# A hybrid encoder layer: inverse softmax sums spread by DMA and applied in attention, instead of by TensorE in the mixing stage

## The chip, the cores and the metric

The kernel runs on one core of one Trainium2 chip. The metric is the device time of one execution in microseconds (us). All data is float32; matmuls are taken as three products of rounded parts (high x high, high x low, low x high) to keep the precision.

## The reference

One layer of a streaming encoder for a prompt of 2048 frames (16 tiles of 128) and a sample group of 8 streams x 16 frames (one more tile). Every sub-layer is wrapped in RMS norms. What matters here is the mixer: half of its channels come from banded attention (8 heads of 64), half from a convolution, and both go through one output projection.

```python
def one_chunk(c):
    ...
    s = jnp.einsum("bqhd,bkhd->bhqk", qc, kc, ...) * scale + bias
    s = jnp.where(valid[None, None, None, :], s, NEG_INF)
    p = jax.nn.softmax(s, axis=-1)
    return jnp.einsum("bhqk,bkhd->bqhd", p.astype(vc.dtype), vc)
...
y = jnp.concatenate([att, c], axis=-1) @ w_out
...
x = x + rmsnorm(y, g_mix_post)      # then memory attention, then a SwiGLU FFN
```

The softmax divides each query's row by the sum of its exponentials. Since the values product is linear, the division can be made after it; the kernel does so for the prompt.

## The kernel before

The engines are TensorE (PE), VectorE (DVE), ScalarE (ACT), GpSimd (POOL), and the DMA queue issued by SyncE (SP). Each engine works through its instructions in one order. That order is set when the program is built: a scheduler simulates all engines with a cost model and gives each engine, at any moment, the ready instruction of highest priority (earlier in the program, mostly). On the chip an instruction whose input isn't there yet holds up everything behind it on its engine. Nearly all on-chip buffers are places at fixed offsets in a few large arenas (`Region().lay(arena, offset in KB, (tag, KB, buffers))`, or `.at(tag, KB, (arena, [offsets]))`); two tiles that share bytes wait for each other as their uses follow in the program.

The stages are: memory keys and values; input projections with the convolution; **attention**; the **mixing stage** (output projection, with the sample's cross-attention filled in between); cross-attention of the prompt; and the FFN.

`attention` walks over 128 units (8 heads x 16 query tiles). For each unit `scores` makes a score tile in PSUM, one DVE instruction (L793) adds the bias and finds the minimum of the negated scores, and ACT (L795) takes the exponential and accumulates the row sums into `self.sums[:, t, h]`, a tile with queries in the partitions. Four units later `transp` transposes the exponentials on PE and splits them into high and low parts; six units later, for each group of four tiles, `values` multiplies by the head's values. Its PSUM result has the channels in the partitions and 512 queries along the row. ACT copies one half out (L900), DVE adds the other and writes the unnormalised result to 64 partitions of `self.attT` (L902). Beside this, generators fill in the sample's attention (`sample`: POOL scales its softmax at L830, PE transposes that at L835), loads of the next head (`head_load`, issued by SP), and the output weights (`out_weights`, L277 and L278 split them).

The sums lie with queries in partitions, but `attT` has them along the row, so they have to be transposed and spread over the 64 channels of a head. Before the change this is done at the mixing stage's pace. `selectors` builds a 16 x 512 matrix of zeros and ones. `weigh(t)` inverts the 8 heads' sums of tile t, splits them into high and low parts (L964 to L967), transposes them on PE (L970) and copies them to SBUF (L973). `prep(t)` in `mixout` then spreads them over the channels by four PE matmuls with the selector (L1015), multiplies `attT` by the result on DVE (L1017), and splits that and the convolution's output `ct` into high and low parts (L1023, L1024). `weigh` runs for tiles 0 and 1 near attention's end, for the others two tiles ahead in the mixing stage.

`mixout` takes the sample tile first, then tiles 0 to 15: 48 matmuls a tile (`mm3h`, L291), k from 0 to 7, of which k = 0 to 3 need the attention half and k = 4 to 7 the convolution half. Its first tiles are prepared with raised priority, so that their matmuls can fill PE at attention's end. Two buffers hold `ct`, loaded by SP (L1008), three PSUM banks the output halves. The last two output weights (k = 6 and 7) take the place of the last head's values, so they are split only after the last `values` matmul.

The places that matter for the change:

```python
# attention's pool: fa is an arena of 32 KB per partition
.lay(fa, 0, ("qbd", 0.5, 2), ("osb", 0.5, 2)).lay(fa, 5, ("otmp", 2, 1), ...)
# mixing stage's pool: ff is the same arena
.at("ct", 2, (ff, [2, 10])).lay(ff, 0, ("an", 2, 1)).lay(ff, 5, ("po", 4, 1))
```

Of the kernel before, what the change touches and what calls it, by code (L numbers as in the profile page):

```python
# [17 lines left out]
P = 128  # L18
D = 1024
KC = D // P  # L20
NPT = 16
S_TILE = 16
H = 8
DH = 64
# [9 lines left out]
NEG = -1e30  # L34
RATE = 1.0
DEPTH = 2
WEIGH = (122, 124)
FROM = 2
F2 = 2
SLAST = NPT * (H - 1) + 4  # L40
# [96 lines left out]
class Build:  # L137
# [81 lines left out]
    def setup(self):  # L219
        nc, A = self.nc, self.A  # L220
        enter = lambda n, **kw: self.ctx.enter_context(self.tc.tile_pool(name=self.nm(n), bufs=1, **kw))
        self.const = enter("const")
        self.dpool = enter("dram", space=DRAM)
        sb, ps = enter("sb"), enter("ps", space=PSUM)
        self.sbF = Arena(sb.tile([P, 13120], F32, tag="f", name="sbf"))
        sbr = Arena(sb.tile([P, 22528], F32R, tag="r", name="sbr"))
        self.xctx = ExitStack()
        sx = self.xctx.enter_context(self.tc.tile_pool(name=self.nm("sx"), bufs=1))
        self.sbR = Joined(sbr, Arena(sx.tile([P, 5120], F32R, tag="x", name="sbx")))
        self.ps = Arena(ps.tile([P, 4096], F32, tag="p", name="psb"))  # L230
# [12 lines left out]
        self.hn = [self.dram(f"hn{g}", [P, 3, 7, 512]) for g in range(3)]  # L243
        self.af = [self.dram(f"af{g}", [P, NF // 2, 7, 3 * P]) for g in range(3)]
        self.vsamp = self.dram("vsampd", [P, 512])

    def bias_tables(self, pool):
        nc, A = self.nc, self.A
# [500 lines left out]
    def att_pools(self):  # L749
# [1 line left out]
        self.attp = (Region().lay(sbF, 34.5, ("kc", 4, 2), ("kt", 4.25, 1), ("pp", 1.5, 1), ("vn", 2, 1))  # L751
                     .at("z", 2.5, (fa, [24]), (fb, [0, 2.5, 5]), (fa, [9, 11.5, 14, 16.5]))
                     .lay(fb, 7.5, ("vc", 4, 2), ("nmx", 0.03125, 12), ("sm", 0.03125, 2))
                     .lay(fa, 0, ("qbd", 0.5, 2), ("osb", 0.5, 2)).lay(fa, 5, ("otmp", 2, 1), ("bs", 1.0625, 1)).lay(fa, 19, ("bt", 2.5, 2))
                     .lay(sbR, 0, ("q20", 8, 1), ("k20", 8, 1), ("kl0", 8, 1), ("q21", 8, 1), ("k21", 8, 1), ("kl1", 8, 1),
                          ("v20", 8, 1), ("ph1", 10, 1), ("pl1", 10, 1), ("v21", 8, 1))
                     .lay(sbR, 88, ("ph0", 10, 1), ("pl0", 10, 1)))
# [25 lines left out]
    def attention(self):  # L783
        nc, A = self.nc, self.A
# [100 lines left out]
                nc.vector.tensor_tensor(pl[:, a:b, :], pt[:, :b - a, :], ph[:, a:b, :].bitcast(F32), ALU.subtract)  # L885
            return quad

        def values(h, hd, t, quad):
            v2 = hd[3]
            po = self.t(ps_o, [P, 4, P], F32, "o")  # L890
            blocks = sorted(range(max(0, t - 4), t + 4), key=lambda j: j > t + 1)
# [1 line left out]
            for x, (src, j) in enumerate(ops):  # L893
# [8 lines left out]
            nc.vector.tensor_tensor(self.attT[rr, h // 2, t * P:(t + 4) * P], po[:DH].rearrange("p a b -> p (a b)"),  # L902
                                    tmp[:, :], ALU.add)

        units = [(h, t) for h in range(H) for t in range(NPT)]
        heads = {0: self.head0}
# [7 lines left out]
            qbds.append(qb)  # L914
        fill = iter(())
        self.wo_load = self.out_weights()
        zq, quads = {}, {}
        n = len(units)
        LT = 4
        LV = 6  # L920
        for i in range(n + LV + 1):
            if i < n:
                h, t = units[i]
# [10 lines left out]
            u = i - LV  # L934
            if 0 <= u < n and u % 4 == 3:
                h, t = units[u]
                values(h, heads[h], t - 3, quads.pop(u // 4))
            if i % NPT and (i % 2 == 0 or i > SLAST):
                next(fill, None)
            if i == n - NPT:  # L940
                self.selectors()
            if i in WEIGH:
                for _ in self.weigh(WEIGH.index(i), ps_t, "t"):
                    pass
            if i in (n - 13, n - 11, n - 9, n - 7):
                next(self.wo_load)

    def selectors(self):

        nc = self.nc  # L950
        pool = self.wp = Region().lay(self.fa, 27.5, ("eye", 0.03125, 1), ("rc", 0.03125, 2)).lay(
            self.sbR, 84, ("expand", 2, 1), ("rt", 0.5, 3), ("rs", 0.0625, 2))
        eye = self.t(pool, [2 * H, H], F32, "eye")
        nc.vector.tensor_tensor(eye[:, :], self.ident[:2 * H, :H], self.ident[:2 * H, H:2 * H], ALU.add)
        expand = self.t(pool, [2 * H, 4, 2, DH], F32R, "expand")
        nc.vector.tensor_copy(expand[:, :, :, :].rearrange("p a b d -> p (a b) d"),
                              eye[:, :].unsqueeze(2).to_broadcast([2 * H, H, DH]))
        self.expand = expand[:, :, :, :].rearrange("p a b d -> p a (b d)")
        self.rts = {}

    def weigh(self, t, ps, tag):
        nc, pool = self.nc, self.wp
        rc = self.t(pool, [P, H], F32, "rc", 2)
        nc.vector.reciprocal(rc[:, :], self.sums[:, t, :])  # L964
        rs = self.t(pool, [P, 2, H], F32R, "rs", 2)
        nc.vector.tensor_copy(rs[:, 0, :], rc[:, :])
        nc.vector.tensor_tensor(rs[:, 1, :], rc[:, :], rs[:, 0, :].bitcast(F32), ALU.subtract)  # L967
        yield
        pt = self.t(ps, [P, 512], F32, tag)
        nc.tensor.transpose(pt[:2 * H, :P], rs[:, :, :].bitcast(F32).rearrange("p a h -> p (a h)"),  # L970
                            self.ident[:, :])
        self.rts[t] = self.t(pool, [2 * H, P], F32R, "rt")
        nc.scalar.copy(self.rts[t][:, :], pt[:2 * H, :P])  # L973

    def out_weights(self):
        nc = self.nc
# [12 lines left out]
    def mixout(self, ctx):  # L989
# [16 lines left out]
        def prep(t):  # L1006
            ct = self.t(pool, [P, 4, P], F32, "ct", 2)
            nc.sync.dma_start(ct[:, :, :].rearrange("p a b -> p (a b)"), self.cs[t])  # L1008
            if t == S_TILE:
                att = self.attS[:, :, :]  # L1010
            else:
                rt = self.rts.pop(t)
                pt = self.t(ps_p, [P, 512], F32, "p")
                for j in range(4):
                    nc.tensor.matmul(pt[:, j * P:(j + 1) * P], self.expand[:, j, :], rt[:, :], start=True, stop=True)  # L1015
                an = self.t(pool, [P, 4, P], F32, "an", 1)
                nc.vector.tensor_tensor(an[:, :, :], self.attT[:, :, t * P:(t + 1) * P],  # L1017
                                        pt[:, :].rearrange("p (j q) -> p j q", q=P), ALU.mult)
                att = an[:, :, :]
            mh = self.t(pool, [P, KC, P], F32R, "mh", 2)  # L1020
            ml = self.t(pool, [P, KC, P], F32R, "ml", 2)
            for sl, src in ((slice(4, 8), ct[:, :, :]), (slice(0, 4), att)):
# [684 lines left out]
```

## Time and profile before

| what | value |
|---|---|
| median of 3 runs | 3013.76 us (3012.63 to 3015.66) |
| the profiled execution's own time | 3012.76 us |
| its span, first to last instruction | 3011.0 us |
| mean granted TensorE clock | 0.991 |
| HBM traffic | 366 MB read, 142 MB written, 169 GB/s over the span |

A span is what the profiler recorded between the first and the last instruction; the execution's time is 1.8 us more. In rows of the timeline the first number is the start in us from the span's start, the second the duration in us; L-numbers are lines of the kernel; `<-` in brackets names what ended the idle time before. PEld is PE's weight load, which overlaps its matmuls. `sbf`, `sbr`, `sbx`, `flexb` are the SBUF arenas, `psb` is PSUM. An entry such as `x16: 188/203/206` gives the count and the minimum, median and maximum duration in ns. A waits entry gives the us in total, the times and the longest.

### The profile page before, as it was taken

Reading aid. Unit: us, or ns where it says so; the run is one execution under the profiler, and the core shown is the slowest. Engines: PE = TensorE matmul, PEld = TensorE weight load, DVE = VectorE, ACT = ScalarE, POOL = GpSimd, SP = SyncE. Lnnn points to the kernel's source line nnn. Section 1 sums busy time; section 2 is a strip of 40 time slices with the busy share of each in tenths; the row PEclk is TensorE's granted clock in tenths of the full one; section 3 lists DMA queues with packets and bytes.
Section 4 is the critical chain, followed back from the end, with each engine's and each line's share of the span. In section 5 each row is a group of like instructions: output and inputs, shape, how many; then the busy total and the mean of one; then the engine's idle time right before and its main releaser. Section 6 shows DMA issues by size and latency. Waiting matters only on the chain.

```text
span 3011.0 us, 46007 instructions
## 1 busy us (share of the span) xinstructions
PE 2925.7 (97%) x16932; PEld 2676.2 (89%) x16932; DVE 2126.8 (71%) x3077; ACT 1354.8 (45%) x2726; POOL 1392.6 (46%) x1304
## 2 busy tenths in 40 slices
PE   8999999979999999999999999999999999999998
PEld 8999999968887887787888999999999999888786
DVE  6696895958885466435358888888788998556655
ACT  4545464658883344323234333433344444433433
POOL 0267495710013235235357565546555776424413
PEclk9999999989999999999999999999999999999999
DMA  8635255557744556324246333544334446756664
GB/s 305 241 112 183 92 162 161 170 153 184 191 132 164 176 194 212 109 75 137 95 151 227 119 136 117 200 156 152 133 136 157 140 144 208 253 174 209 224 198 164
DMA packets 196430, 500.09 MB, mean 166 GB/s; under 512 B 18981, under 2 KB 82989, under 8 KB 187875
## 3 DMA queue, kind: packets, MB, share of 16 engines
q1 hardware_dynamic: 185883, 461.09, 47.8%
q0 software_dynamic: 10320, 36.05, 3.1%
q8 instruction: 133, 2.18, 0.3%
q14 instruction: 94, 0.77, 0.1%
HBM read 365.97 MB, written 141.81 MB: 169 GB/s over the span
## 4 chain that ended last, share of the span: by engine, by line
PE 38%; DMA 4%; POOL 3%; issue 3%; DVE 2%; ACT 1%; SPq 0%; DVEq 0%; POOLq 0%; ACTq 0%
PE psb L285 12%; PE psb L284 12%; PE psb L283 12%; DMA sbf<-in_w_down_dram 2%; POOL sbf L1558 1%; PE psb L291 1%; DMA sbf<-x 1%; PE psb L1413 1%; DVE sbr L1619 0%; POOL sbf L340 0%; DVE sbr L1436 0%; DMA sbf<-in_w_gate_dram 0%; DMA sbf<-hn 0%; DMA hn<-sbf 0%; DVE flexb L1498 0%
## 5 line engine op out<-in xcount | busy, mean ns | idle before, releaser
L283 PE MATMUL psb<-sbr 128*128 128x384 f32 (+3 forms) x2808 | 944.3, 338 | 3.5 <-ACT sbr L319 1.1
L284 PE MATMUL psb<-sbr 128*128 128x384 f32 (+3 forms) x2356 | 807.6, 343 | 2.6 <-DVE sbr L320 2.4
L285 PE MATMUL psb<-sbr 128*128 128x512 f32 (+3 forms) x1848 | 634.3, 345 | 3.7 <-DVE sbr L1619 3.5
L283 PEld LDWEIGHTS psb<-sbr 128*128 128x128 f32 x2808 | 531.4, 190 | 33.5 <-ACT sbr L1618 2.4
L285 PE MATMUL psb<-sbr,sbx 128*128 128x384 f32 (+2 forms) x1484 | 478.3, 323 | 0.1
L284 PEld LDWEIGHTS psb<-sbr 128*128 128x128 f32 x2356 | 446.1, 189 | 29.2 <-DVE sbr L320 2.7
L285 PEld LDWEIGHTS psb<-sbr 128*128 128x128 f32 x1848 | 348.4, 189 | 33.4 <-DVE sbr L1619 6.9
L291 PE MATMUL psb<-sbr 128*128 128x512 f32 x1200 | 297.8, 397 | 4.3 <-POOL sbr L1271 1.5
L1436 DVE TENSOR_TENSOR sbr<-sbf,sbr 128x512 fp32r<-128x512 f32 x258 | 262.6, 1021 | 39.8 <-ACT sbr L1435 38.9
L1435 ACT CAST sbr<-sbf 128x512 fp32r<-128x512 f32 x258 | 159.3, 620 | 276.5 <-PE psb L284 234.6
L285 PEld LDWEIGHTS psb<-sbr,sbx 128*128 128x128 f32 x1484 | 281.4, 190 | 0.6 <-POOL sbx L278 0.4
L523 DVE SCALAR_TENSOR_TENSOR psb<-sbf,psb 128x768 f32<-128x768 f32 (+1 forms) x290 | 264.4, 912 | 6.2
L291 PEld LDWEIGHTS psb<-sbr 128*128 128x128 f32 x1200 | 223.6, 190 | 50.5 <-POOL sbr L1271 1.9
L1619 DVE TENSOR_TENSOR sbr<-sbf,sbr 128x384 fp32r<-128x384 f32 (+1 forms) x231 | 166.5, 743 | 92.6 <-ACT sbr L1618 91.3
L278 POOL TENSOR_TENSOR sbx<-sbf,sbr 128x1024 fp32r<-128x1024 f32 x60 | 152.9, 2551 | 81.3 <-ACT sbr L277 77.7
L1558 POOL TENSOR_TENSOR sbf<-sbf 128x512 f32<-128x512 f32 x77 | 107.6, 1401 | 167.9 <-DMA sbf<-in_w_down_dram 166.2
L1618 ACT CAST sbr<-sbf 128x384 fp32r<-128x384 f32 (+1 forms) x231 | 110.5, 497 | 164.9 <-PE psb L284 133.4
L533 POOL TENSOR_TENSOR flexb<-flexb,flexb 128x128 f32<-128x128 f32 (+1 forms) x180 | 167.1, 929 | 21.7 <-ACT flexb L532 12.1
L283 PE MATMUL psb<-sbr,sbx 128*128 128x384 f32 (+1 forms) x524 | 170.8, 327 | 2.5 <-ACT sbx L1435 1.8
L1435 ACT CAST sbx<-sbf 128x512 fp32r<-128x512 f32 x153 | 94.7, 620 | 163.4 <-PE psb L284 143.2
L1436 DVE TENSOR_TENSOR sbx<-sbf,sbx 128x512 fp32r<-128x512 f32 x153 | 154.5, 1012 | 17.9 <-ACT sbx L1435 17.5
L277 ACT CAST sbr<-sbf 128x1024 fp32r<-128x1024 f32 x98 | 102.5, 1050 | 108.2 <-PE psb L284 56.1
(339 smaller groups left out, 6159.7 us busy)
## 6 DMA issues: line engine op xcount, KB each, us to landing
af<-flexb SPq DMA_DIRECT2D x33, 1344.0 KB, 6.1
sbf<-in_w_down_dram SPq DMA_DIRECT2D x154, 256.0 KB, 3.8
sbf<-af SPq DMA_DIRECT2D x90, 384.0 KB, 3.9
sbf<-in_w_gate_dram SPq DMA_DIRECT2D x66, 512.0 KB, 3.4
sbf<-in_w_up_dram SPq DMA_DIRECT2D x66, 512.0 KB, 3.5
sbf<-x SPq DMA_DIRECT2D x49, 512.0 KB, 4.0
sbf<-in_w_in_dram SPq DMA_DIRECT2D x48, 512.0 KB, 4.2
sbr<-ks SPq DMA_DIRECT2D x28, 512.0 KB, 10.3
```

The source lines that it names most:

```text
L278: self.lo_engine.tensor_tensor(lo[:, :], wf[:, :], hi[:, :].bitcast(F32), ALU.subtract)
L283: nc.tensor.matmul(ps, lh, rh, start=start, stop=False, **kw)
L284: nc.tensor.matmul(ps, lh, rl, start=False, stop=False, **kw)
L285: nc.tensor.matmul(ps, ll, rh, start=False, stop=stop, **kw)
L291: nc.tensor.matmul(y[o], l, r[:, o * 512:(o + 1) * 512], start=start and x == 0, stop=stop and x == 2)
L523: nc.vector.scalar_tensor_tensor(acc if w < CW - 1 else o, src(w), cwt[:, j, w:w + 1], acc, ALU.mult, ALU.add)
L533: nc.gpsimd.tensor_tensor(o, o, v, ALU.add)
L1435: nc.scalar.copy(hs[j][:, :], src[j])
L1436: nc.vector.tensor_tensor(ls[j][:, :], src[j], hs[j][:, :].bitcast(F32), ALU.subtract)
L1558: nc.gpsimd.tensor_tensor(acc[:, :], acc[:, :], q[:, :], ALU.add if s > 0 else ALU.subtract)
L1618: nc.scalar.copy(ch[:, m], a[:, x, m])
L1619: nc.vector.tensor_tensor(cl[:, m], a[:, x, m], ch[:, m].bitcast(F32), ALU.subtract)
```

## The change

`inverse` inverts the four columns of sums of one head and one group of four tiles on DVE (128 x 4), writes them by a DMA to a row in DRAM in query order (512 runs of 4 bytes), and reads that row back by a second DMA into 64 partitions at once (`rb`, 64 x 512). It is called two units after the group's last scores. `values` then has one more instruction: POOL multiplies the 64 x 512 block of `attT` in place by `rb`. There is one `rb` buffer, at 2 KB of `fa`, and two small `rc` buffers at 4 KB. In the mixing stage `prep` takes `attT` as it is; `selectors`, `weigh` and everything that calls them go.

```diff
-WEIGH = (122, 124)
+        self.rec = [self.dram(f"rec{h}", [NPT * P]) for h in range(H)]
-                     .lay(fa, 0, ("qbd", 0.5, 2), ("osb", 0.5, 2)).lay(fa, 5, ("otmp", 2, 1), ...
+                     .lay(fa, 0, ("qbd", 0.5, 2), ("osb", 0.5, 2), ("rb", 2, 1), ("rc", 0.03125, 2)).lay(fa, 5, ("otmp", 2, 1), ...
-        def values(h, hd, t, quad):
+        def values(h, hd, t, quad, inv):
...
-            nc.vector.tensor_tensor(self.attT[rr, h // 2, t * P:(t + 4) * P], po[:DH].rearrange("p a b -> p (a b)"),
-                                    tmp[:, :], ALU.add)
+            att = self.attT[rr, h // 2, t * P:(t + 4) * P]
+            nc.vector.tensor_tensor(att, po[:DH].rearrange("p a b -> p (a b)"), tmp[:, :], ALU.add)
+            nc.gpsimd.tensor_tensor(att, att, inv[rr, :], ALU.mult)
+
+        def inverse(h, t):
+            rc = self.t(pool, [P, 4], F32, "rc", 2)
+            nc.vector.reciprocal(rc[:, :], self.sums[:, t:t + 4, h])
+            row = self.rec[h][t * P:(t + 4) * P]
+            nc.sync.dma_start(row.rearrange("(a p) -> p a", p=P), rc[:, :])
+            rb = self.t(pool, [P, 4 * P], F32, "rb")
+            rr = slice((h % 2) * DH, (h % 2 + 1) * DH)
+            nc.sync.dma_start(rb[rr, :], bass.AP(row.tensor, row.offset, [[0, DH], [1, 4 * P]]))
+            return rb
...
+        LR = 2
...
-                values(h, heads[h], t - 3, quads.pop(u // 4))
+                values(h, heads[h], t - 3, quads.pop(u // 4), invs.pop(u // 4))
+            u = i - LR
+            if 0 <= u < n and u % 4 == 3:
+                invs[u // 4] = inverse(units[u][0], units[u][1] - 3)
...
-            if i == n - NPT:
-                self.selectors()
-            if i in WEIGH:
-                for _ in self.weigh(WEIGH.index(i), ps_t, "t"):
-                    pass
...
-    def selectors(self):
-        ...
-    def weigh(self, t, ps, tag):
-        ...
 # mixout, prep
-                rt = self.rts.pop(t)
-                pt = self.t(ps_p, [P, 512], F32, "p")
-                for j in range(4):
-                    nc.tensor.matmul(pt[:, j * P:(j + 1) * P], self.expand[:, j, :], rt[:, :], start=True, stop=True)
-                an = self.t(pool, [P, 4, P], F32, "an", 1)
-                nc.vector.tensor_tensor(an[:, :, :], self.attT[:, :, t * P:(t + 1) * P],
-                                        pt[:, :].rearrange("p (j q) -> p j q", q=P), ALU.mult)
-                att = an[:, :, :]
+                att = self.attT[:, :, t * P:(t + 1) * P]
...
-            if 0 < i < len(order) - 2:
-                yield from self.weigh(order[i + 2], ps_p, "p")
```

More of the change, by code (lines that the diff above doesn't have):

```diff
@@ L753, in att_pools @@
                      .lay(fb, 7.5, ("vc", 4, 2), ("nmx", 0.03125, 12), ("sm", 0.03125, 2))
-                     .lay(fa, 0, ("qbd", 0.5, 2), ("osb", 0.5, 2)).lay(fa, 5, ("otmp", 2, 1), ("bs", 1.0625, 1)).lay(fa, 19, ("bt", 2.5, 2))
+                     .lay(fa, 0, ("qbd", 0.5, 2), ("osb", 0.5, 2), ("rb", 2, 1), ("rc", 0.03125, 2)).lay(fa, 5, ("otmp", 2, 1), ("bs", 1.0625, 1)).lay(fa, 19, ("bt", 2.5, 2))
                      .lay(sbR, 0, ("q20", 8, 1), ("k20", 8, 1), ("kl0", 8, 1), ("q21", 8, 1), ("k21", 8, 1), ("kl1", 8, 1),
@@ L916, in attention @@
         self.wo_load = self.out_weights()
-        zq, quads = {}, {}
+        zq, quads, invs = {}, {}, {}
         n = len(units)
@@ L936, in attention @@
                 h, t = units[u]
-                values(h, heads[h], t - 3, quads.pop(u // 4))
+                values(h, heads[h], t - 3, quads.pop(u // 4), invs.pop(u // 4))
+            u = i - LR
+            if 0 <= u < n and u % 4 == 3:
+                invs[u // 4] = inverse(units[u][0], units[u][1] - 3)
             if i % NPT and (i % 2 == 0 or i > SLAST):
                 next(fill, None)
-            if i == n - NPT:
-                self.selectors()
-            if i in WEIGH:
-                for _ in self.weigh(WEIGH.index(i), ps_t, "t"):
-                    pass
             if i in (n - 13, n - 11, n - 9, n - 7):
                 next(self.wo_load)
-    def selectors(self):
[L950 to L959, printed above, removed]
-    def weigh(self, t, ps, tag):
[L962 to L973, printed above, removed]
     def out_weights(self):
```

## The prediction

> **What bounds the kernel now.** I read the page first, then windows of the stretch in question, then the groups of that stretch, and last the timeline around single instructions.
>
> ```profile
> PE 2925.7 (97%) x16932; PEld 2676.2 (89%) x16932; DVE 2126.8 (71%) x3077; ACT 1354.8 (45%) x2726; POOL 1392.6 (46%) x1304
> ```
>
> TensorE (PE) is busy for 97% of the span, but that is an average; the change touches two stages only. The windows below (busy us of each engine, then granted clock, DMA share and GB/s) cover attention (about 642 to 926) and the mixing stage (from 898, overlapping, to about 1187).
>
> ```profile
> core 0: us, PE busy (x) PEld busy (x) DVE busy (x) ACT busy (x) POOL busy (x), PEclk, DMA share, GB/s
> ...
> 760.00:800.00 40.00, 39.04 (x296) 34.10 (x288) 35.08 (x85) 34.56 (x83) 2.69 (x6) 1.00 0.69 180
> 800.00:840.00 40.00, 39.85 (x320) 35.56 (x321) 33.41 (x84) 34.74 (x85) 1.49 (x4) 1.00 0.77 190
> ...
> 900.00:925.00 25.00, 24.55 (x137) 20.42 (x135) 15.96 (x28) 10.43 (x21) 5.85 (x4) 1.00 0.33 116
> 925.00:960.00 35.00, 31.38 (x118) 24.71 (x119) 16.85 (x25) 11.72 (x25) 11.26 (x16) 0.85 0.51 162
> ...
> 1080.00:1120.00 40.00, 40.00 (x215) 33.64 (x215) 29.27 (x37) 17.70 (x35) 16.32 (x30) 1.00 0.59 201
> ```
>
> The mixing stage is plainly bound by PE: 40.00 of 40 us, the other engines at three quarters or less, DMA at 0.6. So PE work taken out there is time taken off. Attention is also PE-first (39 to 40 of 40), but DVE and ACT stand at 84 to 88% and the DMA engines at 0.69 to 0.77, while POOL is nearly empty. The seam at 925 to 960 is the one place here with real PE idle time (3.6 us) and a lowered clock (0.85).
>
> **What leaves PE.** The groups of PE between 885 and 1165 us (busy us, mean ns):
>
> ```profile
> L291 PE MATMUL psb<-sbr,sbx 128*128 128x512 f32 x406 | 104.9, 403 | 2.1 <-DVE flexb L1066 2.1
> L1015 PE MATMUL psb<-sbr 16*128 16x128 f32 x64 | 11.0, 286 | 0.2 <-ACT sbr L973 0.2
> L970 PE MATMUL psb<-ident,sbr 128*16 128x128 f32 x16 | 4.4, 272 | 0.0
> ```
>
> and the timeline of PE around one of each:
>
> ```profile
> 1002.20 1.63 PE L291 MATMUL psb<-sbr 128*128 128x512 f32 x6
> 1003.76 0.66 PE L1015 MATMUL psb<-sbr 16*128 16x128 f32 x4
> 1004.34 0.50 PE L291 MATMUL psb<-sbr 128*128 128x512 f32 x1
> ...
> 991.21 3.35 PE L291 MATMUL psb<-sbr,sbx 128*128 128x512 f32 x14
> 994.40 0.27 PE L970 MATMUL psb<-ident,sbr 128*16 128x128 f32 x1
> 994.43 4.59 PE L291 MATMUL psb<-sbr,sbx 128*128 128x512 f32 x19
> ```
>
> Wide matmuls start 0.23 us apart (19 in 4.59 us). The last of the six before the spreading group therefore starts at about 1003.43 and would be followed at 1003.66; the next one comes at 1004.34, so a group of four costs 0.68 us: 16 x 0.68 = 10.9, which agrees with the 11.0 us of the group. The transpose hides in the pipeline: the next wide matmul starts at 994.43 where 994.39 was due, 0.05 us with rounding, 0.8 us for 16. I take 11.8 us off; the two busy times together, 15.4, are the upper end, and 9.5, with the five groups before 930 counted at a third because PE waits there anyway, the lower.
>
> DVE loses 16 each of the scaling, the inverse and two casts in the mixing stage, and ACT 16 copies. I cost that at nothing: PE covers it (DVE 29 of 40 us at most). If PE were not the bound there, scaling and inverse alone (min/median/max ns below) would be worth 16 x (0.683 + 0.203) = 14.2 us.
>
> ```profile
> L1017 DVE TENSOR_TENSOR flexb<-sbf,psb x16: 635/683/689, 908.4 to 1158.2; 128x512 f32<-128x512 f32 x16
> L964 DVE RECIPROCAL flexb<-sbf x16: 188/203/206, 866.7 to 1086.6; 128x8 f32<-128x8 f32 x16
> ```
>
> **What comes into attention.** There are 32 groups of four tiles (8 heads x 4). Each gets an inverse of 128x4 on DVE, two transfers on SP's queue, and one 64x512 product on POOL. The first score reductions of head 1 and of head 7 give a head's length, 179.7 / 6 = 29.9 us, and 1.87 us for one of its 16 units:
>
> ```profile
> 685.12 0.29 DVE L793 CUSTOM_DVE_ANT_0 flexb<-psb,flexb 128x128 f32<-128x128 f32 x1 [0.79 <-PE psb L866]
> ...
> 864.77 0.29 DVE L793 CUSTOM_DVE_ANT_0 flexb<-psb,flexb 128x128 f32<-128x128 f32 x1
> ```
>
> *DVE.* 32 x 0.19 us = 6.1 us on an engine at 84%. PE's longest wait in attention is for DVE:
>
> ```profile
> PE psb L866 <- DVE flexb L793: 10.0, 12, 5.1
> ...
> 671.22 0.44 DVE L793 CUSTOM_DVE_ANT_0 flexb<-psb,flexb 128x272 f32<-128x272 f32 x1 [5.26 <-DMA flexb<-toep]
> ```
>
> Between 0 (hidden by the two score buffers) and 6.1 us; 1.5 taken, since PE idles only some 2% there.
>
> *The transfers.* No row has a run of 4 bytes. Nearest in shape is the value store: 128 partitions x 4 runs of 512 bytes, 2.7 us to landing; one of them keeps the 16 DMA engines at 0.30 for 3 us, 0.9 us. The spread back (64 rows of 2 KB) lies near the 32 KB load with 2 KB rows.
>
> ```profile
> vs<-sbx SPq DMA_DIRECT2D x32, 256.0 KB, 2.7
> ...
> sbf<-vsampd SPq DMA_DIRECT2D x8, 32.0 KB, 3.3
> sbr<-ks SPq DMA_DIRECT2D x28, 512.0 KB, 10.3
> ...
> 201.00:204.00 3.00, 3.00 (x27) 3.00 (x26) 2.93 (x5) 1.84 (x3) 2.84 (x3) 1.00 0.30 87
> ```
>
> A pair thus takes 0.4 + 2.7 + 0.4 + 3.3 = 6.8 us unloaded. From the inverse (two units after a group's last scores) to its values (six) lie four units, 7.5 us: just in time. But each head begins with six loads of 512 KB (the keys land after 10.3 us), and a pair behind them comes some 7 us later (10.3 against 3.3). The sum takes the DMA engines' time of a pair from the store, 0.9 + 0.5 (half the bytes). The Trainium skill ("DMA: Bandwidth & Descriptors", "Specifications") says that under 512 B the engines read, modify and write; that speaks against the change. By it, as an estimate, the first transfer doubles to 1.8 us and the time comes out as in rival 3 below; no run here shows which holds.
>
> *Who waits for a late pair.* The second transfer waits at the head of SP's queue for the first to land and for the product before to leave the one `rb` buffer; behind it stand the loads of the next head, of the sample caches and of the output weights. The heads' loads are issued a whole head ahead: head 2's first keys here, while head 2 begins at about 685.1 + 29.9 = 715 and the keys land in 10.3 us. So SP may stall 10 us and more without harm.
>
> ```profile
> 682.17 0.45 SPq L780 DMA_DIRECT2D sbr<-ks  x1
> ```
>  On POOL the product waits for `rb` and the next instructions queue behind it. The one with little slack is L830, which scales the sample's softmax; PE transposes its result 0.16 us later, in order:
>
> ```profile
> 704.23 0.68 DVE L902 TENSOR_TENSOR sbf<-psb,flexb 64x512 f32<-64x512 f32 x1
> ...
> 707.90 0.97 POOL L830 TENSOR_SCALAR flexb<-flexb 128x272 f32<-128x272 f32 x1 [4.12 <-DVE flexb L829]
> ...
> 709.03 0.49 PE L835 MATMUL psb<-ident,flexb 128*128 128x128 f32 x3
> ...
> L1558 POOL TENSOR_TENSOR sbf<-sbf 128x512 f32<-128x512 f32 x77 | 107.6, 1401 | 167.9 <-DMA sbf<-in_w_down_dram 166.2
> ```
>
> The product itself, at 1.4 us, would run from 704.9 to 706.3 and be gone by then; 32 x 1.4 = 45 us lie in POOL's empty time. Late by 2 to 5 us it holds up PE 8 times: 0 to 20 us, 2 taken.
>
> *DVE against POOL.* The row that could show the two hindering each other:
>
> ```profile
> 900.80 0.69 DVE L1024 TENSOR_TENSOR sbr<-sbf,sbr 128x512 fp32r<-128x512 f32 x1 [0.47 <-PE psb L866]
> 901.04 2.72 POOL L278 TENSOR_TENSOR sbr<-sbf,sbr 128x1024 fp32r<-128x1024 f32 x1 [11.43 <-ACT sbr L884]
> 901.41 2.89 DVE L1024 TENSOR_TENSOR sbr<-flexb,sbr 128x512 fp32r<-128x512 f32 x1
> ...
> L793 DVE CUSTOM_DVE_ANT_0 flexb<-psb,flexb x136: 280/810/826, 643.0 to 904.2; 128x640 f32<-128x640 f32 x96, 128x256 f32<-128x256 f32 x8, 128x128 f32<-128x128 f32 x8, 128x512 f32<-128x512 f32 x8
> ...
> L278 POOL TENSOR_TENSOR sbr<-sbf,sbr 128x1024 fp32r<-128x1024 f32 x4 | 9.9, 2466 | 35.8 <-PE psb L896 14.9 <-ACT sbr L884 11.4 <-PE psb L866 7.2
> ```
>
> A DVE subtraction with both inputs in SBUF took 2.89 us instead of 0.69 while POOL worked; the score reduction, with one input in PSUM, never exceeded 0.826. The Trainium skill ("SBUF — State Buffer", on the shared port pair) says the pair is locked for a whole instruction, also by a DVE operation with two SBUF inputs; the trace agrees. By it attention's DVE work, one input in PSUM, is left alone; if every DVE instruction could be held, 32 x 1.4 = 45 us of DVE would be at stake, and the 0.826 excludes that, for three more of POOL's subtractions (2.4 us each) ran beside those 136. Only the last product, at the seam, meets two-input work: 0 to 1.3 us, 0.6 taken.
>
> **The seam.** This cost isn't named in the change. `rb` lies at 2 to 4 KB of the arena `fa`, exactly where the mixing stage has its first `ct` buffer, that of the sample tile, mixed first. Before, nothing in attention used that place and the load ran ahead:
>
> ```profile
> 671.89 0.33 SPq L1008 DMA_DIRECT2D flexb<-cs  x1
> ...
> 922.60 1.27 PE L896 MATMUL psb<-sbr 128*128 128x512 f32 x7
> ...
> 928.22 4.63 PE L291 MATMUL psb<-sbr 128*128 128x512 f32 x10 [0.69 <-DVE sbr L278]
> ...
> 936.73 7.37 PE L291 MATMUL psb<-sbr,sbx 128*128 128x512 f32 x24 [2.13 <-DVE flexb L1066]
> ```
>
> Now the load has to wait for the last product. From the end of the last values matmul (923.9, call it T): ACT's copy and DVE's sum (0.7 each) to T+1.4; POOL's last weight subtraction (2.4), which waits for the same matmul, to T+2.4; the product to T+3.8, issue 0.4, load 2.7 (as the store of the same 256 KB), ACT's cast 0.6: T+7.5. Before, the sample tile went on at 928.22, T+4.3, with 12 matmuls left (k = 6, 7); now 24 are left (k = 4 to 7), 5.5 us at 0.23, more while the clock is low. PE gets its banks back 3.9 us after their end: T+16.9 to T+19.9, against 936.73 = T+12.9. The 12 matmuls fewer ahead of T bring T forward by 2.8. Loss 1.2 to 4.2, plus up to 2.8 if the tail is not PE-bound and T doesn't move; 4 taken, 1 to 7 kept.
>
> **Sum**, against the profiled execution (3012.76 us: its span of 3011.0 and 1.8 around it; the median of the three runs is 1.0 higher): -11.8 + 1.5 + 2 + 0.6 + 4 = -3.7, and with the median 3010.1. I say 3010. What can be told from no change is 0.2%, 6 us: below 3007.7 is faster, above 3019.8 slower.
>
> **Rivals.**
> 1. *Everything is hidden*: pairs in time, and the tail's matmuls reordered so that `ct` costs its least. 3013.8 - 11.8 + 1.2 + 0.5 = 3004. For it: POOL's emptiness, loads issued a head ahead. Against: the seam's overlap in the code. Chance 0.35.
> 2. *Slower: L830 behind a late product.* From 2 us of lateness of `rb` beyond 706.5 on, PE stops at L835 once a head. At 3 us a head 24 us, with the other terms 3013.8 - 11.8 + 6.1 + 24 = 3032; it decides from about 1.5 us a head (3020). For it: 10.3 us landings. Against: L830 comes late in a head, after the burst. Chance 0.18.
> 3. *Slower: the DMA engines become the bound.* 0.77 of a 29.9 us head is 23.0 us; four pairs at 0.9 + 0.5 make 28.6, still under. If 4-byte runs cost twice a 512-byte run, 32.2: 2.3 us x 7 heads, 3010 + 16 = 3026. Chance 0.09.
> The forecast keeps 0.38.
>
> **How the numbers follow.** The range reaches from rival 1 with a little more taken off PE (3001) to rival 3 and the lower part of rival 2 (3027); it has room for the 2 or 3 us by which a new order of instructions, worked out for the whole program, can differ. Faster takes rival 1 (0.35); slower rivals 2 and 3 (0.27); within 0.2% the forecast.
>
> **What would show it.** In the changed profile: no 16-row matmuls; mixing windows still at 40 of 40, the stage some 8 us shorter from its first full tile on; `flexb<-cs` issued first near the last product instead of at 672; POOL some 45 us more; in attention, PE's waits for L793 slightly longer, and any at L835 new. I am wrong if the `rec` transfers land well past 5 us, if L830 starts right behind a product that waited for a DMA, if PE's idle time in attention grows by over 5 us, or if the seam costs nothing.

## The result, and the profile after

The changed kernel takes 3171.8 us (median of 4 runs, 3168.1 to 3178.3) where the kernel before, on the same chip, takes 3014.4: a ratio of 1.052, 95% interval 1.050 to 1.054. It is slower by some 157 us; 3010 us, and at most 3027, had been forecast. The profiled execution has a span of 3176.2 us, 165.2 more than before.

The windows of attention and of the start of the mixing stage in the changed kernel's trace (busy us of each engine, granted clock, DMA share, GB/s):

```profile
681.00:721.00 40.00, 25.76 (x145) 21.58 (x145) 18.87 (x50) 17.83 (x42) 3.30 (x5) 0.79 0.73 112
...
801.00:841.00 40.00, 32.31 (x214) 28.41 (x215) 26.03 (x66) 24.16 (x57) 6.51 (x8) 0.86 0.75 127
...
961.00:1001.00 40.00, 17.61 (x123) 15.47 (x122) 12.89 (x34) 13.68 (x31) 7.37 (x6) 0.68 0.41 71
...
1161.00:1201.00 40.00, 40.00 (x240) 34.51 (x239) 18.48 (x28) 16.70 (x33) 11.24 (x26) 1.00 0.60 204
```

The mixing stage is as full as it was. In attention PE is busy for 18 to 32 of 40 us (39 to 40 in the rows shown of before), and no other engine has taken its place: DVE and ACT are down too, POOL is nearly empty, and the DMA engines move less (71 to 127 GB/s, where it was 180 and 190) at a share of busy time of 0.73, 0.75 and 0.41 (before 0.69 and 0.77). A stage in which every engine is partly idle and none is full waits for something that takes long and uses little. Two PE lines give the stage's length: the row of the score matmuls, with their first and last start, and the timeline of PE at the seam:

```profile
L866 PE MATMUL psb<-sbr x448: 221/338/690, 641.0 to 1046.3; 128*128 128x384 f32 x72, 128*128 128x256 f32 x68, 128*128 128x128 f32 x7, 128*128 128x512 f32 x3
```

```profile
1077.77 2.08 PE L896 MATMUL psb<-sbr 128*128 128x512 f32 x9
...
1101.98 7.38 PE L291 MATMUL psb<-sbr,sbx 128*128 128x512 f32 x24 [3.67 <-DVE flexb L1041]
```

From the first score matmul to the end of the last values matmul 438.9 us pass; before, 281.8 (642.1 to 923.9). That is +157.1. From there to the mixing stage's second batch of 24 matmuls it is 22.1 us against 12.9: +9.2. All the rest of the program is 1.1 us shorter. So the loss lies in attention. Its waits (us in total, times, longest), between 640 and 1100 us:

```profile
POOL sbf L904 <- DMA flexb<-rec: 108.6, 11, 14.5
DVE flexb L909 <- DMA rec<-flexb: 86.7, 12, 12.6
...
PE psb L883 <- DVE sbx L885: 49.7, 7, 20.1
...
PE psb L835 <- POOL flexb L830: 30.0, 6, 10.3
...
PE psb L896 <- DVE sbf L903: 27.0, 3, 10.3
```

The two longest are waits for the two transfers; PE's three are for DVE and POOL, which stand in them. SP's queue, which is listed apart, stands at the second transfer until the first has landed:

```profile
SPq L914 <- DMA rec<-flexb: 124.1, 11, 15.9
```

One such stop, as the timeline of the changed kernel shows it:

```profile
704.80 0.36 SPq L911 DMA_DIRECT2D rec<-flexb  x1
...
715.77 0.18 DVE L909 RECIPROCAL flexb<-sbf 128x4 f32<-128x4 f32 x1 [11.41 <-DMA rec<-flexb]
715.86 0.65 DVE L903 TENSOR_TENSOR sbf<-psb,flexb 64x512 f32<-64x512 f32 x1
...
716.66 0.76 PE L896 MATMUL psb<-sbx,sbr 128*128 128x512 f32 x1 [10.27 <-DVE sbf L903]
```

The first transfer of a group goes out at 704.80. The inverse of a later group needs one of the two `rc` buffers, and gets it only when an earlier first transfer (here the one issued at 695.11) has landed; DVE stands for 11.4 us, with the sum of the values behind it, and PE behind that. Meanwhile none of the three has work that it can start. The sizes and the landing times of the transfers stand in the DMA issues of the stage (640 to 1100; median us to landing), and in the row of line 911, the first transfer:

```profile
sbr<-ks SPq DMA_DIRECT2D x28, 512.0 KB, 17.2
flexb<-rec SPq DMA_DIRECT2D x32, 128.0 KB, 4.8
rec<-flexb SPq DMA_DIRECT2D x32, 2.0 KB, 13.2
```

```profile
DMA to landing us min/median/max: 10.0/13.2/20.6
```

Two kilobytes take 13.2 us at the median, where the forecast had 2.7. The trace dates only some of the landings, 6 of these 32, so 10.0 is not the least of all: one that is not dated took some 8 us, as shown further down.

### The profile page after: what moved, and what is told of

Read it like the earlier page. It is cut to its first block, busy times and chain, and to the rows that moved or that the text cites. A ratio compares the mean times of both kernels' runs of the same rounds, so it can differ in the third digit from the quotient of the medians.

```text
span 3176.2 us, 46003 instructions
## 1 busy us (share of the span) xinstructions
PE 2952.1 (93%) x16852; PEld 2699.8 (85%) x16852; DVE 2108.3 (66%) x3043; ACT 1357.8 (43%) x2710; POOL 1432.4 (45%) x1336
```

## The experiments

Ratios are to the kernel before on the same chip, with 95% intervals. Line numbers move by a few between kernels: the first transfer is `rec<-flexb`, the second `flexb<-rec` or, where `rb` lies elsewhere, `sbr<-rec`.

**1. Without the transfers.** The edit: one tile of ones in the place of `rb`, and no call of `inverse`.

```
-                invs[u // 4] = inverse(units[u][0], units[u][1] - 3)
+                invs[u // 4] = ones          # 1.0, in rb's place
```

> This kernel is the changed one without its inverses and transfers: rb is filled once with ones, so the rows are multiplied by 1 and the softmax stays undivided; POOL's 32 products, the place of rb and the lighter mixing stage stay. Four theories for the 157 us. W (writes): the transfer in 4-byte runs lands after 10 to 21 us where I had put 2.7, and all that waits for it (DVE for an rc buffer, SP for the second transfer, POOL for rb) sets attention's pace. B (buffers): the slow write would do no harm if DVE didn't wait for one of two rc buffers. S (SP): the harm is that SP stands at the second transfer and the loads of the next head come late. N: it isn't the transfers but the products on POOL, the place of rb or the new order of instructions. W, B and S all expect 3003 to 3011 us here (11.8 off PE, 1 to 7 back at the seam); N expects over 3100.

Measured: 3014.3 us, ratio 0.9999 (0.9987 to 1.0011). The 157 us are gone, with 32 products still on POOL: the product, PE's order and the buffers' places are not what costs. But the time is that of the kernel before, not 3003 to 3011; where PE's saving went is question 4.

**2. Which wait?** Three edits of the changed kernel, one wait or one shape each:

```
e2:  -  rc = self.t(pool, [P, 4], F32, "rc", 2)          (region: "rc", 0.03125, 2)
     +                                                   (region: "rc", 0.03125, 16)
e3:  -  nc.sync.dma_start(row.rearrange("(a p) -> p a", p=P), rc[:, :])   # 512 runs of 4 B
     +  nc.sync.dma_start(row.rearrange("(p a) -> p a", a=4), rc[:, :])   # 128 runs of 16 B
        (and the product reads rb with a stride of 4)
e4:  both transfers on nc.gpsimd's queue instead of nc.sync's
```

> The changed kernel with 16 rc buffers instead of 2, so that DVE's inverse no longer waits for an earlier write to land. B expects nearly everything back: 3010 to 3040 us. W expects that only DVE's own wait goes (87 us of it in the list of waits, partly in parallel with others), while SP and POOL still wait: 3060 to 3140. S expects no change to speak of: 3150 and more.

> The changed kernel with the inverses written in the order in which they lie: 128 runs of 16 bytes instead of 512 of 4, the same 2 KB; the row is read back as before, and the product reads it with a stride of four. Number of transfers, buffers, queue and order of waits stay as they are. W expects the write to land in 3 to 6 us and 3005 to 3035 us in all. B expects the same only if landing is under the 14 us between inverses two apart, so no difference from W here. S, where the count of transfers and the stop on SP matter, expects the loss to shrink by less than half: over 3080. N expects about 3170, or more, since the product's read is strided.

> The changed kernel with both small transfers issued from POOL's queue instead of SP's; runs of 4 bytes and buffers as they are. S expects 3010 to 3050 us, since the loads are never behind a waiting transfer. W expects the landing to stay above 8 us and POOL to stand in SP's place, with L830 and the products behind it: 3120 to 3250. B expects DVE's wait for rc to stay and the time above 3100.

Measured: e2 3178.2 us (1.0542, 1.0505 to 1.0580), e3 3050.2 (1.0119, 1.0096 to 1.0142), e4 3188.6 (1.0577, 1.0536 to 1.0617). In e2 DVE's wait is gone from the list, and nothing is won (theory W had expected 3060 to 3140 us); its waits read

```profile
POOL sbf L904 <- DMA flexb<-rec: 143.8, 16, 14.5
...
PE psb L835 <- POOL flexb L830: 100.0, 6, 24.3
```

The same lateness comes out one step later: POOL waits longer for `rb`, L830 stands behind it, and PE waits for L830. In e4 the same waiting moves to POOL's own queue (73.7 us for the first transfers to land). So neither the two buffers nor SP's queue alone is the cause. The shape of the first transfer is: with a quarter of the runs it lands in 5.7 us (median) and 122 of the 157 us are back, though not all that theory W had expected (3005 to 3035 us).

**3. Load or lateness?** In e8 the first transfers are there, but nobody reads them and nothing waits for them (16 `rc` buffers; the products take constant ones). In e7 all is there, but the product comes one group later.

```
e8:  inverse() writes rec and returns the tile of ones; no second transfer
e7:  -  values(...)                    # ends with the product of this group
     +  late.append(values(...)); if len(late) > 1: weigh(*late.pop(0))
     both: 16 rc buffers, rb in 4 KB of sbR that nothing else uses
```

> The inverses and the first transfers (512 runs of 4 bytes) alone: nobody reads what they write, the products use constant ones (rows are not scaled by the sums), 16 rc buffers, ones in the unused 4 KB. Theory L: nothing waits for them, so the time is that of e1b plus DVE's 32 inverses, 3003 to 3015 us, though ks lands late. Theory C: 3060 to 3170 us, most of the loss of the changed kernel, since the loads behind and beside the writes come late.

> Runs of 4 bytes as in the changed kernel, but the product of a group is issued one group later (behind the next group's values, some 7.5 us more lead), with 16 rc and two rb buffers in the unused 4 KB. Theory L (lateness: the 162 us are engines that wait for a landing): most of it is hidden, 3003 to 3030 us, POOL's wait for rb under 30 us in all, DVE's none. Theory C (contention: the 512 runs hold up the DMA engines, and the loads of keys and tables with them): 3080 to 3170 us even so, with PE's waits for data of ks and toep.

Measured: e8 3073.6 us (1.0194, 1.0173 to 1.0215), e7 3192.4 (1.0584, 1.0557 to 1.0610). e8 falls into the lower end of theory C's range, e7 lies above both ranges. The bare transfers cost about 62 us against the same kernel without them (3011.1, below), though nobody waits for them: that is load. The rest of the loss, some 95 us, comes only where the transfers are read and waited for, and more time for the product alone does not help. (The two parts need not be the same in the changed kernel, where the DMA engines are busy for 65.6% of 640 to 1100 us; in e8 it is 99.9% of a stretch shown below.) The trace of e7 has the reason in SP's own waits:

```profile
SPq L917 <- DMA rec<-flexb: 285.5, 29, 14.7
```

In 29 of 32 groups SP stands at the second transfer until the first has landed. I then moved the second transfer a group later in the program as well (e10, and e11 with 16-byte runs).

```
e10, e11:  spread(h, row), the second transfer, is called beside the group's values, not in inverse()
```

> Runs of 4 bytes; the second transfer is issued one group after the first (beside that group's values, 7.5 us later), and the product another group after it; 16 rc and two rb buffers in the unused 4 KB. Theory Q (queue: each second transfer holds SP's queue until the first has landed, 10 to 13 us for a group every 7.5 us, and with it the next pair and the heads' loads): the stall goes and only the load on the DMA engines is left, as in the run with the writes alone: 3065 to 3100 us, with SP's waits for rec in the tens of us where e7 had 285. If the lateness of the product was the point, e7 would have helped already; if it is the transfers themselves in any order, 3150 to 3190 us.

> The same order as e10 with 128 runs of 16 bytes, which land in 5.7 us, under a group's 7.5. Theory Q: no stall of SP's queue is left, and little load: 3008 to 3022 us, as the kernel before or a little better. If runs of 16 bytes still load the DMA engines so that the keys come late, 3025 to 3040 us as e6.

Measured: e10 3189.9 us (1.0575, 1.0556 to 1.0594), e11 3034.0 (1.0060, 1.0041 to 1.0079). e10 did not test what it was meant to. Its SP wait is 285.5 us again, because the scheduler still put each second transfer ahead of the next group's first one, as this stretch of SP's queue in e10 shows:

```profile
726.83 0.45 SPq L920 DMA_DIRECT2D sbr<-rec  x1
727.37 0.54 SPq L914 DMA_DIRECT2D rec<-flexb  x1
...
737.64 0.45 SPq L920 DMA_DIRECT2D sbr<-rec  x1
...
738.82 0.42 SPq L914 DMA_DIRECT2D rec<-flexb  x1
```

First and second transfers take turns, so that one group cannot pass in less than one landing: 10 us and more, where attention has a group every 7.5. Only an explicit order parts them (e13; e14 with 16-byte runs):

```
e13, e14:  with self.tc.issue_after(<first transfer of the next group>):
               rbs[g] = spread(...)
```

> Runs of 4 bytes. e10 did not test theory Q: its trace shows each second transfer issued directly ahead of the next group's first one, so that the two still take turns on SP's queue, and SP waits 285 us for rec as in e7. Here each second transfer is put behind the next group's first transfer on the queue (and the product a group later), so that two first transfers land at the same time. Theory Q: SP's wait for rec falls from 285 us to under 130, the attention stage comes down to that of the writes alone: 3065 to 3110 us. If the queue is not what costs the other 100 us: 3150 to 3190 us again.

> The order of e13 with 128 runs of 16 bytes. Theory Q: SP hardly waits for rec any more (100 us in e11), and the time is that of the 16-byte writes alone (3019) and a little for the second transfers: 3016 to 3026 us. If SP's wait in e6 and e11 was harmless and the 20 us are load on the DMA engines by both transfers: 3030 to 3037 us.

Measured: e13 3127.7 us (1.0370, 1.0352 to 1.0389), e14 3031.4 (1.0056, 1.0035 to 1.0077).

```profile
SPq L917 <- DMA rec<-flexb: 110.5, 20, 11.5
```

SP's wait falls from 285.5 to 110.5 us, as expected, and the time by 62 us against e10: the turn-taking on SP's queue is worth that much in e10's order. Of e10's 116 us over the bare transfers (3073.6), 54 are left, and the time is 18 us above the range of theory Q. The second transfers' own load can be some 12 us of them, as an estimate from 16-byte runs (e14 against e12's bare first transfers, 3019.2 us). e13's waits still have POOL at 97.3 us for `rb` and PE at 53.6 for L830: its first transfers now land in 17.0 us (median). With 16-byte runs the order is worth next to nothing: e11 and e14 miss theory Q's ranges and lie in those of its rivals.

**4. The seam.** e1 again, with the ones in unused space and not where the mixing stage has its first `ct` buffer.

```
-  .lay(fa, 0, ("qbd", 0.5, 2), ("osb", 0.5, 2), ("rb", 2, 1), ("rc", 0.03125, 2))
+  .lay(fa, 0, ("qbd", 0.5, 2), ("osb", 0.5, 2), ("rc", 0.03125, 2))
+  .lay(sbR, 84, ("rb", 2, 2))
```

> As e1 (products with constant ones, no inverse, no transfer; the sums are left out), but the ones lie in 4 KB of sbR that nothing else uses, so that the mixing stage's first ct buffer is free during attention again. Seam theory: PE's saving of 11.8 us was there in e1 and was given back at the seam, where the sample tile's ct load and split came after attention: e1b takes 3003 to 3008 us against the kernel before, ct<-cs is issued far ahead of 900 again, and PE starts the second batch of 24 wide matmuls within 13 us of the last values matmul (21 us in e1). If the saving was never there, 3012 to 3016 as e1.

Measured: 3011.1 us (0.9987, 0.9976 to 0.9998). PE at the seam in e1, then in e1b, and e1b's first load of `ct` on SP's queue:

```profile
923.38 1.83 PE L896 MATMUL psb<-sbr 128*128 128x512 f32 x10
...
946.74 7.27 PE L291 MATMUL psb<-sbr,sbx 128*128 128x512 f32 x24 [3.62 <-DVE flexb L1043]
```

```profile
927.25 1.83 PE L896 MATMUL psb<-sbr 128*128 128x512 f32 x10
...
941.66 7.36 PE L291 MATMUL psb<-sbr,sbx 128*128 128x512 f32 x24 [2.41 <-DVE flexb L1043]
```

```profile
673.80 0.33 SPq L994 DMA_DIRECT2D flexb<-cs  x1
```

The load goes out at 673.8 again, and the second batch starts 12.6 us after the last values matmul instead of 21.5. So in these two traces sharing the place costs 8.9 us at the seam. The runs' medians differ by only 3.2 us and their intervals overlap; attention itself ends 4 us later in e1b (its order is another one). The time lies between the ranges of the two theories.

**5. What makes the first transfer slow?** Five kernels with first transfers that nobody reads, all with constant ones in the products (so nothing is scaled by the sums), differ only in the runs' shape and place; e17 is the changed kernel itself with its runs apart (its second transfers read other bytes than the sums).

```
e8:   512 runs of 4 B, side by side             row.rearrange("(a p) -> p a", p=P)
e12:  128 runs of 16 B, side by side            row.rearrange("(p a) -> p a", a=4)
e15:  128 runs of 4 B, side by side             row[0:P] <- rc[:, 0:1]
e16:  512 runs of 4 B, 512 B apart              row.rearrange("(a p k) -> p a k", ...)[:, :, 0:1], k = 128
e18:  512 runs of 4 B, 64 B apart               the same with k = 16
e17:  the changed kernel, first transfer as in e16
```

> The inverses and the first transfers alone as 128 runs of 16 bytes, read by nobody (the products use constant ones, so rows are not scaled by the sums). If the load on the DMA engines goes by the number of runs: a quarter of the 62 us that 512 runs cost, 3020 to 3030 us. If it is a fixed latency that nobody waits for: 3008 to 3016 us, as e1b.

> Writes alone, as e12 (products by constant ones; only one of a group's four columns is written, and nobody reads it): 128 runs of 4 bytes instead of 128 of 16. If the number of runs sets the cost, landing and time are those of e12: 3015 to 3026 us, landing 5 to 8 us. If a run of 4 bytes costs more than one of 16: 3030 us and more, landing 9 us and more.

> Writes alone, as e8 (512 runs of 4 bytes, products by constant ones), but each run goes to a 512-byte stretch of DRAM of its own instead of beside the next. If the number of runs sets the cost: as e8, 3065 to 3085 us, landing 10 us or more. If the runs hinder each other because they fall in the same stretch of DRAM: 3010 to 3040 us, landing under 6 us.

> Writes alone, as e16 (products by constant ones, nobody reads what is written), with the 512 runs 64 bytes apart instead of 512: eight runs share 512 bytes. If what they must not share is 64 bytes: as e16, 3014 to 3024 us, landing 3 to 5 us. If it is 512 bytes: between e16 and e8, 3030 to 3065 us, landing 6 us and more.

> The changed kernel itself, in the same order and with the same buffers, but the 512 runs of 4 bytes go 512 bytes apart. The second transfer reads the first 2 KB of the stretch, as many bytes in as many rows as before (they hold rows of a cache, copied there at the start by 8 small transfers, worth up to 4 us; so attention's rows are scaled by these and not by the sums). Theory D (runs that fall in the same 512 bytes hinder each other, and everything else follows from the late landing): landing of the first transfer 3 to 6 us, 3020 to 3055 us, like e3 with its 16-byte runs. If the number of runs or the order on SP's queue costs by itself: 3100 us and more.

Measured: e12 3019.2 us (1.0013, 1.0004 to 1.0023), e15 3052.0 (1.0120, 1.0094 to 1.0146), e16 3018.8 (1.0013, 1.0000 to 1.0026), e18 3017.0 (1.0005, 0.9996 to 1.0015), e17 3048.7 (1.0107, 1.0087 to 1.0127). e12 lies between its two ranges; the other four came as the theory of neighbours (for e15: that a run of 4 bytes costs more than one of 16) had it. From the same stretch of each, 700 to 900 us, the queue's packets, MB and share of the 16 DMA engines' time, and the first transfers' count, size and median landing; in order e1b (no transfers), e8, e16, e15:

```profile
q1 hardware_dynamic: 8218, 33.96, 65.7%
```

```profile
q1 hardware_dynamic: 19863, 33.18, 99.9%
...
rec<-flexb SPq DMA_DIRECT2D x22, 2.0 KB, 17.0
```

```profile
q1 hardware_dynamic: 21812, 33.53, 71.9%
...
rec<-flexb SPq DMA_DIRECT2D x25, 2.0 KB, 3.6
```

```profile
q1 hardware_dynamic: 11099, 32.76, 94.8%
...
rec<-flexb SPq DMA_DIRECT2D x23, 0.5 KB, 13.7
```

e8 and e16 send the same 512 runs of 4 bytes. Side by side they fill the DMA engines to 99.9% and land in 17.0 us; 512 bytes apart they take 71.9% and land in 3.6. And 128 runs of 4 bytes, a quarter of the packets, are nearly as bad (94.8%, 13.7 us) when all of them lie in 512 bytes. So it is not the number of runs, and not their 4 bytes alone, but that runs of 4 bytes are close neighbours. 64 bytes apart is already far enough (e18: the whole stage's landing has a median of 4.0 us, like e16's 3.8), though eight runs then share 512 bytes. Side by side, 16 runs of 4 bytes share each 64 bytes; with 4 runs of 16 bytes in them (e12) the landing is 3.8 us. From which distance on, between 4 and 64 bytes, runs of 4 bytes no longer disturb each other was not tried, and what happens inside the memory these runs do not show.

e17 carries this over to the changed kernel: its order, buffers and second transfers, only the runs apart, and 123 of the 157 us are gone. (Its profile dates no landing.) Its waits:

```profile
SPq L916 <- DMA rec<-flexb: 66.3, 11, 10.5
...
POOL sbf L906 <- DMA flexb<-rec: 45.3, 9, 10.7
```

What is left in e17 is what e3 had left (34 and 36 us); pairs that are still late behind the heads' loads, the seam and the load of both transfers can each have a part in it. With two `rb` buffers outside `ct` and 16-byte runs it is 20 us:

```
e6:  e3 with 16 rc buffers, ("rb", 2, 2) at sbR 84
```

> 128 runs of 16 bytes as in e3, with 16 rc buffers, and two rb buffers in the unused 4 KB of sbR, so that the second transfer does not wait for the product before it and ct is loaded ahead again. If e3's remaining 36 us are the waits for the one rb buffer and the seam: 3003 to 3020 us. If they are the bare lateness of the landing (5.7 + 3.0 us behind the heads' loads, against a lead of 7.5 us): 3030 to 3045, with POOL L904 still waiting some 40 us for the rb transfer.

Measured: 3034.9 us (1.0056, 1.0034 to 1.0078), in the range that the lateness gave; POOL still waits 46.0 us for the second transfer. But that this lateness is what costs the last 20 us isn't shown: e11 gives the product a group more of lead, e14 also halves SP's wait for the first transfer (55.0 us in its fastest run, 110.1 in e6), and their ratios (1.0060 and 1.0056) are no better than e6's. Load of both transfers, for which e14's expectation had 3030 to 3037 us, fits all three times, but no run separates it; the cause of these 20 us stays open. No version with transfers beats the kernel before. Even e1b, which sends none and computes no inverse, is ahead by 0.1% only.

## Why the prediction was wrong

**The first transfer: the step that failed.** "A pair thus takes 0.4 + 2.7 + 0.4 + 3.3 = 6.8 us unloaded ... just in time" took the landing of 512 runs from the value store, whose 512 runs have 512 bytes each. The count of runs was the same, and the count was not what mattered. The store's runs are longer than 64 bytes; of the new ones 16 lie in 64 bytes. Measured, the landing is 13.2 us at the median, and some 8 us even when the DMA engines have nothing else to do. In this stretch of the changed kernel (672.6 to 681 us in 40 slices, busy tenths of the DMA engines) two first transfers are alone. Their packets are over within some 2 us (the one busy slice later is the fetching of instructions), and the second transfer still goes out only at 680.72, when a first one has landed:

```profile
DMA  0065083000000000000000000000000090000000
...
q1 hardware_dynamic: 1056, 0.00, 6.0%
q8 instruction: 1, 0.02, 2.6%
```

```profile
672.16 0.91 SPq L911 DMA_DIRECT2D rec<-flexb  x2
680.72 0.45 SPq L914 DMA_DIRECT2D flexb<-rec  x1
```

The prediction said it had no row with a run of 4 bytes, and then kept no upper end for the landing: the range was drawn from the DMA engines' time (0.9 us, at most doubled), and the landing stayed at one row's value. Its own signs of being wrong came: landings well past 5 us, L830 right behind products that had waited, PE idle in attention. Alone, as above, a first transfer takes 0.25 us of all DMA engines (half of 6.0% of 8.4 us), far less than 0.9; under load that time came out as 3.0 us. As an estimate from the rows of 700 to 900 us: e1b moves 33.96 MB in 131.4 us, so e8's 33.18 MB are worth 128.4 of its 199.8 us; the other 71.4 belong to some 24 transfers ((13183 - 1068) packets under 512 bytes / 512). For e16 the same sum gives 0.5. The Trainium skill ("DMA: Bandwidth & Descriptors", "Specifications") has read-modify-write below 512 B. The runs of e16 and e18 are below it and cost 0.5 to 0.7 us; so that rule, by which I had doubled the price, does not tell the costly case from the cheap one here.

**"So SP may stall 10 us and more without harm."** Wrong as a rule, though each stall by itself is that short. A queue on which first and second transfers take turns passes one pair in each landing; 32 groups at 10 to 14 us do not fit into 32 x 7.5. I asked how late one load may be, and not how many pairs the queue can pass. e13 shows 62 us for it, against e10; in the changed kernel SP stands there for 124.1 us in 11 waits, and what that alone costs was not measured. With a landing of 2.7 us the step would probably have held.

**DVE was costed without its new wait.** I gave the 32 inverses 1.5 us for their duration (0.18 us each, as measured). But the inverse writes a buffer that a transfer reads, and so waits for a landing two groups back: 86.7 us in the changed kernel. e2 shows that removing it alone moves the wait to POOL, so it was a missing step and not the cause.

**Rival 2's mechanism came, at another price.** L830 behind a late product, PE's wait at L835: 2 us in the sum, 24 in the rival, 30.0 in the trace (100.0 in e2). Both its place and what it starts from were in the prediction; its size hung on the landing. (The rival's sum also leaves out the 4 us of the seam.)

**Rival 3** (the DMA engines become the bound) is what e8 shows, at 99.9%. By its own formula with 3.0 us in the place of 0.9 (23.0 + 4 x (3.0 + 0.5) = 37.0 against 29.9) it gives 7.1 x 7 = 50 us; e8 has 62 without second transfers. In the changed kernel the engines are not full (65.6%, above).

**The seam was there and twice as large.** Forecast 4 (1 to 7), measured 9.2 in the changed kernel, 8.9 by e1 against e1b; of that the whole times of e1 and e1b show only 3.2. The load of `ct` was issued at 1064.41, near the last products, as said; PE's second batch came 22.1 us after the last values matmul, where T+16.9 to T+19.9 had been worked out.

**PE's saving was priced right.** There are no 16-row matmuls left. From the mixing stage's second batch to the first transposes of the next big stage, whose row is

```profile
L1413 PE MATMUL psb<-ident,sbf x252: 221/272/332, 1572.9 to 2291.2; 128*128 128x128 f32 x112, 64*128 64x64 f32 x14
```

```profile
L1388 PE MATMUL psb<-ident,sbf x252: 221/272/446, 1733.9 to 2453.1; 128*128 128x128 f32 x112, 64*128 64x64 f32 x14
```

before and after, it is 636.2 us before (936.73 to 1572.9), 631.9 after (from 1101.98), and 628.1 and 628.8 in e1 and e1b (to 1574.8 and 1570.5). All four do the same matmuls there but for the ones that went, so 4 to 8 us are gained. Of the 16 groups of spreading matmuls 12 lie in that stretch (four, and not five, came earlier), so that by the prediction's own prices 12 x (0.68 + 0.05) = 8.8 us could be gained. e1 and e1b have nearly all of it, the changed kernel half. What keeps e1b from being faster as a whole is attention: it takes 286.5 us there (642.6 to 929.1), and 281.8 before, though e1b has none of the new transfers. PE waits 14.3 us for the score reductions (L793) there, 10.0 before; why is open, since none of the reductions lasts longer (0.826 us at most in both).

**Not tested:** the 0.6 us for DVE and POOL hindering each other, and the cost of the inverses without their transfers. The second can't be large: e18, which has the inverses and writes that land in 4 us, is 6 us above e1b.

## What to carry to other kernels

Price a small transfer by its landing, and by a row whose runs lie in memory as the new ones do: 512 scattered values may land in 4 us, the same values packed side by side in 13. Where one transfer waits on a queue for another, count how many such pairs the queue can pass in the stage, not only how late one may be. And when a cover is thin (a lead of 7.5 us for a pair of 6.8), the landing time needs an upper end in the range, since every buffer, queue and engine behind it turns late at the same point.

## What the runs showed of the hardware

Writes of 4 bytes to DRAM hinder each other when they lie side by side, 16 in 64 bytes: 17.0 us to landing and 3.0 us of all DMA engines (an estimate) for 512 of them, 13.7 and about 2.4 for 128 in 512 bytes; 64 or 512 bytes apart, 4 us and 0.5 to 0.7. While such writes run, other loads slow down with them (the keys' 512 KB land in 16.5 us in e8, 10.7 in e1b), and the engines count as busy for 99.9% of the time and not 65.7% while they move about the same bytes (33.18 and 33.96 MB). When such transfers have the DMA engines to themselves, their packets are over after 2 us and the landing comes at 8, so that the share of the DMA engines does not show the wait. Last, PE's granted clock was lower where PE was idle: 0.68 in the window in which PE was busy for 17.61 of 40 us and 1.00 where it was full. Which of the two comes first no run here shows.
